# Sums of the first projection on VectorE, the fourth product's input in two halves, other banks for the values' upper half

## The chip, the cores and the metric

One core of one Trainium2 chip runs one program. The metric is the device time of one execution in microseconds (us), as the median of several runs. A row of the trace gives times from the start of the profiled execution's span.

## The reference, cut to what matters

A decoder block on 1024 tokens of width 1024: a projection, attention with forgetting and a spatial gate side by side, an output projection, then a gated MLP with a convolution. The change lies in the first quarter, where the projections are made and the gate begins:

```python
xn = rmsnorm(h, norm_mix_g)
proj = xn @ w_in                      # q, k, v (512 each), u, vg (512 each), 8 forget columns
uv = jax.nn.gelu(proj[..., V_END:G_END])
u, vg = uv[..., :512], uv[..., 512:]
vg = rmsnorm(vg, v_gain)              # per group of 64
mixed = einsum('gij,bnjgd->bnigd', tril(w_s), vg) + b_s
sg = u * mixed
```

## The kernel before, in words

**Arithmetic.** A matrix product in float32 is made from three products in a faster format: each operand is split into a high part (a rounded copy, made by ScalarE) and a low part (the operand less the high part, made by VectorE), and TensorE adds high by high, high by low and low by high. `split_w` makes such a pair of a weight, `own` and `hl_of` make it of the tokens' side; `tsplit` (L246) takes a buffer from a ring of six (`ring`, two buffers named wy and four named whl) and splits into it.

**The first projection** (columns u and vg) splits tokens and columns into halves and needs seven products instead of eight. They run one after another: B11, B21, then T2, T3, T1, T4 and B22. A product is 48 matmuls: four blocks `k` of the summed dimension, four blocks of tokens (a PSUM bank each) and three parts. `tmul` issues the twelve of one `k`. The operands called T2, T3, T1 and T4 are sums and differences of blocks: on the tokens' side made from `tmp`, on the weights' side in `sum23` (VectorE), `sum4` (GpSimd) and a loop of four GpSimd additions over `gb`. T3 is the fourth product counted from B11. Between B21 and T2 the value columns are multiplied for the first half of the tokens (`values_low`, eight groups of twelve matmuls, 264 columns wide); after B22 they are multiplied for the other half (`values_high`, the same size, for 256 value columns and the 8 forget columns). Later in the program the other 256 value columns follow (VH for the second half of the tokens, VL for the first).

**PSUM.** There are eight banks, four under the tag "b" (`bank`) and four under "s" (`sbank`). The seven products take them in turn by fours, under the names B and S; `values_high` gets four new "s" banks. `ut[1]` is the last result of B22: VectorE reads it out of the "s" banks (L478, `ut[1] = B[m] - ut[1]`), and only then are these banks free again. In the four steps of the query and key projections (`qk_step`, `product`), `psq` gives tags a and b to "b" banks, c and d to "s" banks.

**Other work beside the products.** The mean squares of the tokens' rows come from eight loads of `xtok`, in turn into one buffer named t01 and one named pt, with a square on ScalarE behind each. t01 is first free when `own("T1", ...)` has read it. From the sums come `rstd1`, and then the gelus of `ut` and `vgt`, the gate's squares, and `gate_norm`.

**Second half of the value columns and the gate's start.** `w0` holds the split weights. The order is VH T3, VL B21, `head_loads(0)` (loads of the first attention head, the last of which needs the buffer of the B21 tokens), VL B11, evacuation of VL, `kept(1)` (load of the values kept in memory since `values_high`, and their evacuation by `evac_v` into tiles named V, which take the buffers of the B11 tokens), VH B22, and `spatial()`: it splits the spatial weights into `ws` (both tiles named wy), evacuates VH, loads the table for Exp, and multiplies the eight groups of the gate, in four banks.

**What sets the order.** A scheduler orders each engine's instructions by the program's order and its own estimate of when each is ready, and gives out buffers and waits. The class `Line` overrides it: while `act.on` and `dve.on` are set, ScalarE and VectorE each run their instructions strictly in the program's order; later ones come behind the last of these. `after`, `behind` and `seq` add single orders. Instructions recorded through `Line` show L51 while the order is on and L44 when it is off, so those line numbers are helpers'. L259 is the matmul of `tmul`, L365 the loads of xtok, L720 to L722 the gate's matmuls, L744 transposes of the gated output, L328 and L353 the GpSimd sums.

Of the kernel before, what the change touches and what calls it, by code (L numbers as in the profile page):

```python
# [14 lines left out]
P = 128  # L15
# [50 lines left out]
def block_kernel(ctx: ExitStack, tc: tile.TileContext, xT, xtok, wuv, wv0, wv1, wqk, cpk, bfv,  # L66
# [16 lines left out]
    def nm(s):  # L83
        uid[0] += 1
        return f"{s}_{uid[0]}"
# [103 lines left out]
    def xr(n, k):  # L189
        return RAW[n][k // 2][:, k % 2, :]  # L190
# [8 lines left out]
    def ring(dt=F32R, n=512):  # L199
        rn[0] += 1  # L200
        return sb(RTAG[(rn[0] - 1) % 6], [P, 2, n], dt)

    def psq(tag):
        return psa.tile([P, 512], F32, tag="b" if tag in "ab" else "s", bufs=4, name=nm("q" + tag))

    def own(n, src, k, row):

# [35 lines left out]
    vgt = [sb("G", [P, 4, 512]) for _ in range(2)]  # L243
    ut = [sb("A", [P, 4, 512]) for _ in range(2)]

    def tsplit(src, gate=None, n=512):  # L246
        w = ring(n=n)
        d = split_w(src, (w[:, 0], w[:, 1]))
        if gate:
            behind(d, gate)  # L250
        return w

    def tmul(banks, w, n, k, first, apart=False, ms_=range(4), own=True):

        ops = [(m, c) for m in ms_ for c in range(3)]
        for m, c in sorted(ops, key=lambda o: (o[1] > 0, o)) if apart else ops:
            ms = slice(m * P, (m + 1) * P)
            xi, wi = ((0, 0), (0, 1), (1, 0))[c]
            pe.matmul(banks[m], xs(n, xi, k)[:, ms], w[:, wi, :], start=(first and k == 0 and c == 0 and (own or m % 2 == 0)),  # L259
                      stop=(k == 3 and c == 2), skip_group_check=True)  # L260
# [30 lines left out]
    def keep(banks, hf):  # L291
        t = ring(F32).rearrange("p a (b c) -> p (a b) c", c=256)
        for m in range(4):
            act.copy(t[:, m, :], banks[m][:, 0:256])
            act.copy(zf[:, 4 * hf + m, 0:8], banks[m][:, 256:264])
        sp.dma_start(out=vd[hf], in_=t)
# [16 lines left out]
    for m in range(4):  # L313
        dve.tensor_tensor(out=ut[0][:, m, :], in0=S[m], in1=vgt[0][:, m, :], op=ALU.add)
    values_low(3)
    act.on = dve.on = False

    s2 = []

    def sum23(k):  # L320
        a11, a21, a22 = ua[k][:, 0, :], gb[k][:, 0, :], gb[k][:, 1, :]
        s2.append(sb("gg", [P, 512]))
        dve.tensor_tensor(out=a11, in0=a21, in1=a11, op=ALU.add)
        dve.tensor_tensor(out=s2[k], in0=a11, in1=a22, op=ALU.add)

    def sum4(k):
        a12 = ua[k][:, 1, :]
        return pool.tensor_tensor(out=a12, in0=s2[k], in1=a12, op=ALU.add)  # L328

    sum23(0)  # L330
    sum23(1)
    for k in range(4):
        tmul(S, tsplit(s2[k]), "T2", k, True)
        s4 = sum4(k)
        if k < 2:
            sum23(k + 2)
    keep(B, 0)
    B, S = S, B

    for j in range(2):  # L340
        t1, t2, t3 = tmp[j]
        for c in range(2):
            k = 2 * j + c
            dve.scalar_tensor_tensor(out=t3[:, c], in0=xr("x12", k), scalar=gk(k), in1=t3[:, c],
                                     op0=ALU.mult, op1=ALU.subtract)
    XS["B22"] = xset(("t3", "t2"))
    for k in range(4):
        own("B22", xr("x22", k), k, 4 + k)
    XS["T3"] = xset(("x1", "x2"))
    for j in range(2):  # L350
        hl_of("T3", j, tmp[j][2])
    for w in gb:
        after(tc, pool.tensor_tensor(out=w[:, 0, :], in0=w[:, 0, :], in1=w[:, 1, :], op=ALU.add), s4)  # L353
    tprod(S, lambda k: ua[k][:, 0, :], "T3", True)
    for m in range(4):
        dve.tensor_tensor(out=ut[1][:, m, :], in0=B[m], in1=vgt[0][:, m, :], op=ALU.subtract)
    XS["T1"] = xset(("H", "H"))
    for j in range(2):
        for c in range(2):
# [11 lines left out]
    sp.dma_start(out=rb, in_=rbd.rearrange("a b -> (a b)").unsqueeze(0).to_broadcast((P, 1024)))  # L371

    tprod(B, lambda k: gb[k][:, 0, :], "T1", True)
    for m in range(4):
        dve.tensor_tensor(out=vgt[1][:, m, :], in0=ut[1][:, m, :], in1=S[m], op=ALU.add)
    for j in range(2):
# [79 lines left out]

    gate_part(1, 0)
    gate_part(1, 2)
    S = [sbank() for _ in range(4)]

    def values_high(k):
        t = wh[k]
# [46 lines left out]
    def forget_sums(c, r):  # L509
        bfb, z, e = c[:, 136:144], c[:, 144:208], c[:, 208:272]  # L510
        tri, ones, lh, ll = r[:, 0:P], r[:, P:2 * P], r[:, 256:320], r[:, 320:384]
        v3 = lambda t: t.rearrange("p (h t) -> p h t", h=8)
        dve.tensor_tensor(out=v3(z), in0=zf[:, :, 0:8].rearrange("p t h -> p h t"),
                          in1=rstd1.unsqueeze(1).to_broadcast((P, 8, 8)), op=ALU.mult)
        dve.tensor_tensor(out=v3(z), in0=v3(z), in1=bfb.unsqueeze(2).to_broadcast((P, 8, 8)), op=ALU.add)
        dve.scalar_tensor_tensor(out=e, in0=z, scalar=-1.0, in1=z, op0=ALU.mult, op1=ALU.max)
        act.activation(e, e, AF.Exp, scale=-1.0)
        act.activation(e, e, AF.Ln, bias=one[:, 0:1])
        dve.tensor_scalar(out=z, in0=z, scalar1=-1.0, scalar2=0.0, op0=ALU.mult, op1=ALU.max)
        dve.tensor_tensor(out=z, in0=z, in1=e, op=ALU.add)  # L520
        dve.tensor_copy(lh, z)
        dve.tensor_tensor(out=ll, in0=z, in1=f32(lh), op=ALU.subtract)
        yield
        ps = sbank()
        for o, m in ((64, tri), (128, ones)):
            pe.matmul(ps[:, o:o + 64], m, lh, start=True, stop=False)
            pe.matmul(ps[:, o:o + 64], m, ll, start=False, stop=True)
        whole, run = v3(ps[:, 128:192]), v3(e)
        dve.memset(run[:, :, 0:1], 0.0)
        for tt in range(1, 8):  # L530
            dve.tensor_tensor(out=run[:, :, tt:tt + 1], in0=run[:, :, tt - 1:tt], in1=whole[:, :, tt - 1:tt], op=ALU.add)
        dve.tensor_tensor(out=v3(z), in0=v3(ps[:, 64:128]), in1=run, op=ALU.add)

        yield
        pe.transpose(ps[0:64, 192:320], z, ident)
        rows = c[0:64, 272:400]
        act.activation(rows, ps[0:64, 192:320], AF.Copy, scale=-1.0)
        sp.dma_start(out=ncr.rearrange("h (t p) -> (h t) p", p=P), in_=rows)
        yield
# [92 lines left out]
        sp.dma_start(out=t, in_=wv1[k])  # L632
        wvr.append(t)

    w0 = [tsplit(wvr[k].rearrange("p a b -> p (a b)"), "keys" if k < 2 else "queries") for k in range(4)]


    gate_gain(0)
# [24 lines left out]
                                 in1=f32(v[:, :, 0, :]), op0=ALU.mult, op1=ALU.subtract)  # L663

    def kept(hf):
        t = ring(F32).rearrange("p a (b c) -> p (a b) c", c=256)
        sp.dma_start(out=t, in_=vd[hf])
        for j in range(4):
            if j % 2 == 0:
                V.append(sb("V", [P, 2, 8, 2, 64], F32R))  # L670
            evac_v(4 * hf + j, 0, t[:, j, :])
# [28 lines left out]
        splits[:] = [split_w(wr, (w[:, 0], w[:, 1]), hi, "pool")]  # L700
        return w

    def spatial():

        wr = sb("pt", [P, 8, P])
        sp.dma_start(out=wr, in_=wsp)
        pool.affine_select(out=wr, in_=wr, pattern=[[0, 8], [1, P]], compare_op=ALU.is_ge,
                           fill=0.0, base=0, channel_multiplier=-1)
        ws = [sb("wy", [P, 8, P], F32R) for _ in range(2)]
        act.on = dve.on = True  # L710
        split_w(wr, ws)

        act.activation(pad[:, 0:1], eps, AF.Exp)
        for m in range(4):
            evac_v(4 + m, 1, VH[m])
        tmp = [sb("pt", [P, 4, 256]) for _ in range(2)]
        for g in range(8):
            c, j = g // 2, g % 2
            ps = bank()
            pe.matmul(ps, ws[0][:, g, :], vgs[c][:, 0, j], start=True, stop=False)  # L720
            pe.matmul(ps, ws[0][:, g, :], vgs[c][:, 1, j], start=False, stop=False)
            m = pe.matmul(ps, ws[1][:, g, :], vgs[c][:, 0, j], start=False, stop=True)  # L722
            v3 = lambda t: t.rearrange("p (t d) -> p t d", d=64)
            u = [ut[hf][:, :, g * 64:(g + 1) * 64] for hf in range(2)]
            dve.scalar_tensor_tensor(out=u[0], in0=v3(ps[:, 0:256]), scalar=bs[:, g:g + 1], in1=u[0],
                                     op0=ALU.add, op1=ALU.mult)
            t = tmp[g // 4][:, g % 4, :]

            def second():
                act.activation(t, ps[:, 256:512], AF.Identity, bias=bs[:, g:g + 1])  # L730
                x = pool.tensor_tensor(out=u[1], in0=v3(t), in1=u[1], op=ALU.mult)
                after(tc, x, splits[0])

            if g < 7:
                second()
        seq(m)
        return second

# [35 lines left out]
    for k in range(4):  # L774
        tmul(VH, a1[k], "T3", k, True, own=False)
    for k in range(4):
        tmul(VL, w0[k][:, :, 256:512], "B21", k, True, own=False)
    for k in range(4):
        pool.tensor_tensor(out=wvr[k][:, 1, :], in0=wvr[k][:, 0, :], in1=wvr[k][:, 1, :], op=ALU.add)
    loads, rows = [None] * 8, [None] * 8  # L780
# [20 lines left out]

    head_loads(0)
    for k in range(4):
        tmul(VL, a1[k], "B11", k, False)
    for m in range(4):
        evac_v(m, 1, VL[m])
    kept(1)
    for k in range(4):
        tmul(VH, tsplit(wvr[k][:, 1, :], n=256), "B22", k, False)
    whs, wrs = [], sg_load(0)  # L810
    for s in range(2):
        after(tc, sp.dma_start(out=ncd[s].rearrange("h (t p) -> (h t) p", p=P), in_=sums[1 + s]), queued[0])
# [836 lines left out]
```

## Time and profile before

| what | value |
|---|---|
| median of 3 runs | 1078.75 us (1078.75 to 1079.66) |
| profiled execution, its own time | 1078.43 us |
| its span, first to last instruction | 1076.7 us |
| TensorE clock granted, mean | 0.992 |
| busy: TensorE, weight loads, VectorE, ScalarE, GpSimd | 98%, 82%, 83%, 53%, 23% |

A row of the timeline gives start, length, engine, line, operation, output<-inputs, shapes and count; in brackets stands the idle time before it and what ended it. Rows of several instructions (x24) are merged. A matmul's end is modelled, so consecutive rows of TensorE are read by their starts. PE is TensorE, DVE VectorE, ACT ScalarE, POOL GpSimd, and SPq the queue from which most transfers are issued.

### The profile page before, as it was taken

The page shows a single profiled execution, that of the slowest core. Times are in us where ns is not written, and L with a number is a line of the kernel's source. Part 1 is how long each engine was busy: PE and PEld are TensorE (multiplying, and loading weights), DVE is VectorE, ACT ScalarE, POOL GpSimd, SP SyncE. Part 2 cuts the span into 40 slices and gives each one's busy share as a digit, 9 for nine tenths or more (in the row PEclk, how much of TensorE's full clock was granted, in tenths as well). Part 3 has the DMA queues.
Part 4 walks back from the last instruction along what each step waited for, and adds up shares of the span by engine and source line. Part 5 has one row for each costly group of instructions (what it writes and reads, how often), then busy time and mean ns, then how long its engine had stood idle before and what let it go on. Part 6 is the DMA issues. An engine that isn't in the chain of part 4 may idle for free.

```text
span 1076.7 us, 14627 instructions
## 1 busy us (share of the span) xinstructions
PE 1054.3 (98%) x5156; PEld 885.6 (82%) x5156; DVE 888.9 (83%) x1291; ACT 571.8 (53%) x1015; POOL 247.6 (23%) x185
## 2 busy tenths in 40 slices
PE   9898999989999999999999999999999999999997
PEld 7877888978898987887888888888888888888886
DVE  6986697876777868999899999989988776898774
ACT  6468544465767755754444444444444444454653
POOL 0502232340402551044333333333322000000000
PEclk9989999999999999999999999999999999999999
DMA  9054166736656345232244513323331899433442
GB/s 339 38 163 132 61 167 175 220 103 189 181 157 181 117 155 180 75 117 98 98 137 153 178 66 132 98 94 103 108 112 45 289 332 313 125 98 96 141 125 96
DMA packets 67184, 155.78 MB, mean 145 GB/s; under 512 B 9028, under 2 KB 9748, under 8 KB 67112
## 3 DMA queue, kind: packets, MB, share of 16 engines
q1 hardware_dynamic: 65800, 154.82, 44.9%
q8 instruction: 40, 0.66, 0.3%
q14 instruction: 32, 0.26, 0.1%
q10 hardware_dynamic: 1312, 0.04, 0.1%
HBM read 111.96 MB, written 42.87 MB: 144 GB/s over the span
## 4 chain that ended last, share of the span: by engine, by line
PE 84%; DVE 8%; DMA 3%; ACT 3%; issue 2%; SPq 0%; POOL 0%; ACTq 0%; DVEq 0%; POOLq 0%
PE k L1499 19%; PE qa L1241 11%; PE qc L1241 10%; PE qd L1241 10%; PE qb L1241 5%; PE pb L938 3%; PE ps L259 3%; PE pb L919 3%; PE qa L406 2%; PE qc L406 2%; PE qd L406 2%; PE pl L879 2%; PE pl L880 2%; PE pf L963 1%; PE pf L965 1%
## 5 line engine op out<-in xcount | busy, mean ns | idle before, releaser
L1499 PE MATMUL k<-whb,wha 128*128 128x512 f32 x924 | 209.7, 389 | 0.0
L1499 PEld LDWEIGHTS k<-whb,wha 128*128 128x128 f32 x924 | 173.4, 188 | 36.2 <-DVE wha L161 0.2
L1241 PE MATMUL qc<-xT,whb 128*128 128x512 f32 x540 | 129.9, 389 | 0.5 <-DVE u L1352 0.5
L1241 PE MATMUL qa<-xB,wha 128*128 128x512 f32 x528 | 127.2, 390 | 0.0
L1241 PEld LDWEIGHTS qc<-xT,whb 128*128 128x128 f32 x540 | 101.2, 188 | 22.1 <-DVE u L1352 0.9
L1241 PEld LDWEIGHTS qa<-xB,wha 128*128 128x128 f32 x528 | 98.8, 188 | 20.8 <-DVE wha L161 0.4
L155 ACT CAST wha<-sg 128x512 fp32r<-128x512 f32 x77 | 47.8, 622 | 96.8 <-PE k L1499 86.3
L155 ACT CAST whb<-sg 128x512 fp32r<-128x512 f32 x82 | 50.5, 617 | 86.8 <-PE qc L1241 68.3
L161 DVE TENSOR_TENSOR wha<-sg,wha 128x512 fp32r<-128x512 f32 x77 | 52.7, 687 | 41.6 <-ACT wha L155 41.5
L920 ACT CAST pt<-pb 128x512 fp32r<-128x512 f32 (+1 forms) x80 | 42.2, 544 | 43.1 <-PE pb L919 34.3
L1241 PE MATMUL qd<-xB,whb 128*128 128x512 f32 x264 | 63.9, 390 | 0.1
L1241 PE MATMUL qd<-xT,whb 128*128 128x512 f32 x264 | 63.6, 389 | 0.0
L1128 POOL TENSOR_TENSOR sg<-raw 128x512 f32<-128x512 f32 x20 | 30.1, 1506 | 136.3 <-DVE whb L161 75.7
L161 DVE TENSOR_TENSOR whb<-sg,whb 128x512 fp32r<-128x512 f32 x82 | 57.7, 704 | 4.4 <-ACT whb L155 4.3
L1241 PE MATMUL qb<-xT,whb 128*128 128x512 f32 x252 | 60.8, 389 | 0.0
L921 DVE TENSOR_TENSOR pt<-pb,pt 128x512 fp32r<-128x512 f32 (+1 forms) x80 | 48.8, 634 | 12.3 <-ACT pt L920 11.0
L1241 PEld LDWEIGHTS qd<-xB,whb 128*128 128x128 f32 x264 | 49.5, 188 | 10.7 <-DVE h L1360 0.5
L1241 PEld LDWEIGHTS qd<-xT,whb 128*128 128x128 f32 x264 | 49.6, 188 | 10.3
L1241 PEld LDWEIGHTS qb<-xT,whb 128*128 128x128 f32 x252 | 47.3, 188 | 9.8
L938 PE MATMUL pb<-pt,V 128*128 128x256 f32 x320 | 52.1, 287 | 0.3 <-DVE pt L921 0.2
L1131 POOL TENSOR_TENSOR sg<-sg,raw 128x512 f32<-128x512 f32 x20 | 33.3, 1665 | 64.2 <-DVE whb L161 64.2
L1129 POOL TENSOR_TENSOR sg<-sg,raw 128x512 f32<-128x512 f32 x20 | 34.9, 1744 | 50.7 <-issue 48.8
(399 smaller groups left out, 2311.1 us busy)
## 6 DMA issues: line engine op xcount, KB each, us to landing
raw<-wup SPq DMA_DIRECT2D x44, 512.0 KB
sg<-hx SPq DMA_DIRECT2D x77, 256.0 KB
hx<-hs SPq DMA_DIRECT2D x44, 256.0 KB
hx<-ca SPq DMA_DIRECT2D x35, 256.0 KB
xT<-wdn SPq DMA_DIRECT2D x28, 256.0 KB
x<-kd SPq DMA_DIRECT2D x24, 256.0 KB
raw<-wqk SPq DMA_DIRECT2D x8, 512.0 KB
qd<-G SPq DMA_DIRECT2D x16, 256.0 KB
```

The costliest lines, as they stand in the source:

```text
L155: act.copy(h, src)
L161: return eng.tensor_tensor(out=l, in0=src, in1=f32(h), op=ALU.subtract)
L259: pe.matmul(banks[m], xs(n, xi, k)[:, ms], w[:, wi, :], start=(first and k == 0 and c == 0 and (own or m % 2 == 0)), stop=(k == 3 and c == ...
L406: pe.matmul(ps, w[:, wi, ks], xs(n, xi, k), start=(first and c == 0), stop=(c == 11), skip_group_check=True)
L919: seq(pe.transpose(ptr[:, c:c + P], tj[jj][:, k * P:(k + 1) * P], ident))
L920: casts.append(act.copy(pt[:, 0, 0:w], ptr[:, 0:w]))
L921: los.append(dve.tensor_tensor(out=pt[:, 1, 0:w], in0=ptr[:, 0:w], in1=f32(pt[:, 0, 0:w]), op=ALU.subtract))
L938: seq(pe.matmul(po[0][:, oo:oo + n], lhs, pt[:, s, o:o + n], start=(k == 0 and s == 0), stop=(s == 1 and half)))
L1129: pool.tensor_tensor(out=s[1], in0=s[0], in1=a11, op=ALU.add)
L1131: pool.tensor_tensor(out=s[3], in0=s[1], in1=a12, op=ALU.add)
L1241: pe.matmul(ps, w[:, wi, ks], xb[:, xi, k, :], start=(first and n == 0), stop=(n == 11), skip_group_check=True)
L1499: pe.matmul(banks[bk + m], xh[:, xi, ms], wh[:, wi, :], start=(first and p_ == 0 and n == 0), stop=(p_ == NP - 1 and n == 2), skip_group_c ...
```

## The change

It has five parts.

1. `sum4` and the four sums of `gb` go from GpSimd to VectorE. `sum4` of the first two `k` comes between the T2 weights, that of the others behind T1's weights; the `gb` sums come behind T3.
2. The strict order of ScalarE and VectorE, which ended after `values_low(3)`, now lasts until T3's weights are split. T3's token side (`third`) is made in two halves, each directly ahead of its two weights; the tokens' side of B22, which was made ahead of T3, is made there too.
3. `values_high` and the forget gate's sums take "b" banks instead of "s"; in `psq` the two tags change places.
4. VL B11 now runs ahead of VL B21.
5. The load of `kept(1)` goes to a buffer named G; the splitting of the spatial weights is taken out of `spatial` and put, with `kept(1)`, ahead of the evacuation of VL; in `spatial`, VH's last two evacuations come behind the first two groups, and the Exp table's load behind VH's first two.

```diff
     def psq(tag):
-        return psa.tile([P, 512], F32, tag="b" if tag in "ab" else "s", bufs=4, name=nm("q" + tag))
+        return psa.tile([P, 512], F32, tag="s" if tag in "ab" else "b", bufs=4, name=nm("q" + tag))
...
-    def tsplit(src, gate=None, n=512):
-        w = ring(n=n)
+    def tsplit(src, gate=None, n=512, tag=None):
+        w = sb(tag, [P, 2, n], F32R) if tag else ring(n=n)
...
     values_low(3)
-    act.on = dve.on = False
...
     def sum4(k):
         a12 = ua[k][:, 1, :]
-        return pool.tensor_tensor(out=a12, in0=s2[k], in1=a12, op=ALU.add)
-
-    sum23(0)
-    sum23(1)
-    for k in range(4):
-        tmul(S, tsplit(s2[k]), "T2", k, True)
-        s4 = sum4(k)
-        if k < 2:
-            sum23(k + 2)
-    keep(B, 0)
-    B, S = S, B
-
-    for j in range(2):
+        dve.tensor_tensor(out=a12, in0=s2[k], in1=a12, op=ALU.add)
+
+    def third(j):
         t1, t2, t3 = tmp[j]
         for c in range(2):
             k = 2 * j + c
             dve.scalar_tensor_tensor(out=t3[:, c], in0=xr("x12", k), scalar=gk(k), in1=t3[:, c],
                                      op0=ALU.mult, op1=ALU.subtract)
-    XS["B22"] = xset(("t3", "t2"))
-    for k in range(4):
-        own("B22", xr("x22", k), k, 4 + k)
-    XS["T3"] = xset(("x1", "x2"))
+        if not j:
+            XS["B22"] = xset(("t3", "t2"))
+        for c in range(2):
+            own("B22", xr("x22", 2 * j + c), 2 * j + c, 4 + 2 * j + c)
+        if not j:
+            XS["T3"] = xset(("x1", "x2"))
+        hl_of("T3", j, tmp[j][2])
+
+    sum23(0)
+    sum23(1)
+    tmul(S, tsplit(s2[0]), "T2", 0, True)
+    tmul(S, tsplit(s2[1]), "T2", 1, True)
+    for k in (2, 3):
+        sum4(k - 2)
+        sum23(k)
+        tmul(S, tsplit(s2[k]), "T2", k, True)
+    keep(B, 0)
+    B, S = S, B
     for j in range(2):
-        hl_of("T3", j, tmp[j][2])
-    for w in gb:
-        after(tc, pool.tensor_tensor(out=w[:, 0, :], in0=w[:, 0, :], in1=w[:, 1, :], op=ALU.add), s4)
-    tprod(S, lambda k: ua[k][:, 0, :], "T3", True)
+        third(j)
+        for k in (2 * j, 2 * j + 1):
+            tmul(S, tsplit(ua[k][:, 0, :]), "T3", k, True)
+    act.on = dve.on = False
     for m in range(4):
         dve.tensor_tensor(out=ut[1][:, m, :], in0=B[m], in1=vgt[0][:, m, :], op=ALU.subtract)
+    for w in gb:
+        dve.tensor_tensor(out=w[:, 0, :], in0=w[:, 0, :], in1=w[:, 1, :], op=ALU.add)
...
     tprod(B, lambda k: gb[k][:, 0, :], "T1", True)
+    sum4(2)
+    sum4(3)
...
-    S = [sbank() for _ in range(4)]
+    S = [bank() for _ in range(4)]
     def values_high(k):
...
-        ps = sbank()
+        ps = bank()
...
-    w0 = [tsplit(wvr[k].rearrange("p a b -> p (a b)"), "keys" if k < 2 else "queries") for k in range(4)]
+    w0 = [tsplit(wvr[k].rearrange("p a b -> p (a b)"), "keys" if k < 2 else "queries", tag="whl") for k in range(4)]
...
     def kept(hf):
-        t = ring(F32).rearrange("p a (b c) -> p (a b) c", c=256)
+        t = sb("G" if hf else "wy", [P, 4, 256])
...
-    def spatial():
-
+    def spatial_weights():
         wr = sb("pt", [P, 8, P])
...
         ws = [sb("wy", [P, 8, P], F32R) for _ in range(2)]
+        split_w(wr, ws)
+        return ws
+
+    def spatial():
+
         act.on = dve.on = True
-        split_w(wr, ws)
-
+        for m in range(2):
+            evac_v(4 + m, 1, VH[m])
         act.activation(pad[:, 0:1], eps, AF.Exp)
-        for m in range(4):
-            evac_v(4 + m, 1, VH[m])
...
             if g < 7:
                 second()
+            if g in (0, 1):
+                evac_v(6 + g, 1, VH[2 + g])
...
     for k in range(4):
-        tmul(VL, w0[k][:, :, 256:512], "B21", k, True, own=False)
+        tmul(VL, a1[k], "B11", k, True, own=False)
...
     head_loads(0)
     for k in range(4):
-        tmul(VL, a1[k], "B11", k, False)
+        tmul(VL, w0[k][:, :, 256:512], "B21", k, False)
+    kept(1)
+    ws = spatial_weights()
     for m in range(4):
         evac_v(m, 1, VL[m])
-    kept(1)
     for k in range(4):
-        tmul(VH, tsplit(wvr[k][:, 1, :], n=256), "B22", k, False)
+        tmul(VH, tsplit(wvr[k][:, 1, :], n=256, tag="whl"), "B22", k, False)
```

## The prediction, made before the changed kernel was run

> **What bounds the kernel now.** I read the page first, then TensorE's waits up to 240 us, its timeline there, the clock by stretches, and the other engines' timelines around each wait.
>
> ```profile
> PE 1054.3 (98%) x5156; PEld 885.6 (82%) x5156; DVE 888.9 (83%) x1291; ACT 571.8 (53%) x1015; POOL 247.6 (23%) x185
> ```
>
> TensorE is busy almost throughout; a gain must come out of its few waits. All of any size before the end lie where the change is made:
>
> ```profile
> PE pb L259 <- ACT x L44: 3.0, 1, 3.0
> PE ps L259 <- DVE A L44: 2.9, 1, 2.9
> PE pb L720 <- ACT pt L51: 2.5, 1, 2.5
> PE pb L259 <- DVE whl L44: 1.5, 1, 1.5
> PE pb L722 <- DVE wy L51: 1.0, 1, 1.0
> ```
>
> In order: T3's tokens, the banks of the values' upper half, banks in the gate, T3's weights, the gate's weights. A wait costs more than its length where the clock falls behind it:
>
> ```profile
> 106.00:108.00 2.00, 2.00 (x11) 1.82 (x10) 1.97 (x4) 1.17 (x3) 2.00 (x2) 0.54 0.00 0
> 220.00:222.00 2.00, 0.96 (x6) 0.46 (x4) 1.97 (x4) 0.00 (x0) 0.00 (x0) 1.00 1.02 203
> ```
>
> The columns are the stretch, its length, five engines' busy time, the granted clock, the DMA share and GB/s. After the 2.9 us wait the clock is 0.54; the 1.0 us wait at 221 leaves it at 1.00. TensorE's rows give each place its cost:
>
> ```profile
> 39.97 5.60 PE L259 MATMUL ps<-whl,H 128*128 128x512 f32 x24
> 45.41 5.60 PE L259 MATMUL ps<-wy,H 128*128 128x512 f32 x24
> 54.00 0.50 PE L259 MATMUL pb<-whl,x 128*128 128x512 f32 x1 [3.00 <-ACT x L44]
> 55.99 10.95 PE L259 MATMUL pb<-whl,x 128*128 128x512 f32 x35 [1.48 <-DVE whl L44]
> 69.49 2.88 PE L259 MATMUL ps<-wy,H 128*128 128x512 f32 x12
> 99.41 2.88 PE L259 MATMUL ps<-wy,t 128*128 128x512 f32 x12
> 105.17 2.13 PE L259 MATMUL ps<-wy,x 128*128 128x264 f32 x9 [2.88 <-DVE A L44]
> 117.24 1.60 PE L259 MATMUL ps<-whl,t 128*128 128x264 f32 x12
> 118.68 2.93 PE L406 MATMUL qa<-V,whl 128*128 128x512 f32 x12
> 213.16 5.92 PE L259 MATMUL ps<-whl,t 128*128 128x256 f32 x48
> 218.92 0.40 PE L720 MATMUL pb<-H,wy 128*128 128x512 f32 x1
> 225.70 0.79 PE L720 MATMUL pb<-H,wy 128*128 128x512 f32 x1 [2.53 <-ACT pt L51]
> 230.09 1.91 PE L744 MATMUL ps<-ident,A 128*128 128x128 f32 x16
> ```
>
> By the starts, 24 matmuls take 45.41 - 39.97 = 5.44 us, a product 10.88. T2 ends at 45.41 + 5.44 = 50.85, T1 begins at 69.49: T3 takes 18.64, which is 7.8 too long. B22 ends at 99.41 + 2.72 = 102.13. A group of the values' upper half takes 118.68 - 117.24 = 1.44, eight take 11.5; they took 118.68 - 105.17 = 13.5, so the slow clock cost 2.0 besides the 2.9. The gate's 24 matmuls, 5.44 at full speed, take from 218.92 to 230.09, 11.2. So 7.8 + 4.9 + 5.7 = 18.4 us is the most to be had.
>
> **The change part by part. T3.** VectorE and GpSimd before:
>
> ```profile
> 44.84 6.82 POOL L353 TENSOR_TENSOR G<-G 128x512 f32<-128x512 f32 x4
> 32.98 1.28 DVE L44 TENSOR_TENSOR raw<-G,raw 128x512 f32<-128x512 f32 x2
> 43.65 1.78 DVE L44 SCALAR_TENSOR_TENSOR pt<-t,g,pt 128x512 f32<-128x512 f32 x1
> 54.12 1.21 DVE L44 TENSOR_TENSOR x<-pt,x 128x1024 fp32r<-128x1024 f32 x1
> 58.80 2.47 DVE L44 TENSOR_TENSOR A<-ps,G 128x512 f32<-128x512 f32 x4
> 62.52 1.40 DVE L44 SCALAR_TENSOR_TENSOR H<-t,g,H 128x512 fp32r<-128x512 f32 x2
> 50.56 1.33 ACT L44 ACTIVATE t<-x,g 128x512 fp32r<-128x512 f32 x2 [3.25 <-DVE G L44]
> 52.90 1.04 ACT L44 CAST x<-pt 128x1024 fp32r<-128x1024 f32 x1 [1.01 <-DVE t L44]
> ```
>
> A three-operand step takes 1.78 us beside GpSimd's additions and 0.70 (half of 1.40) without them. An addition takes 0.6 on VectorE (1.28 for two, pipelined), 1.7 on GpSimd. So moving the sums shortens what stands beside them. In the strict order VectorE goes on at 32.98. Four sums and two low parts bring it to about 36.9 (estimate, with the waits for ScalarE's high parts). Two rounds of `sum4`, two sums, a high part (0.65) and a low part are 3.3 each: 43.5. Each half of T3 is then 1.4 (two steps), 0.8 (ScalarE's first scaled copy), 1.4 (two low parts of B22's tokens), 1.1 (the 1024 copy), 1.2 (its low part) and 1.2 (two weights) = 7.1: 50.6 and 57.7. The first half is there when T2 ends at 50.85. The second half's first weight is complete at 57.2 where TensorE wants it at 50.85 + 5.44 = 56.3: a wait of about 1.0, too short for the clock by the row at 221. T3 ends at 62.7, 6.8 earlier.
>
> **T1, a new wait.** Before T1's first low part VectorE still has T2's readout (2.4 by the row at 58.80), the `gb` sums that GpSimd did unseen (2.4), four low parts of T1's tokens (2.8, by 62.52) and the weight (0.6). From 57.8 that is 66.0. TensorE waits about 3.1 us and, by the 2.9 us wait above, loses 2.0 more to the clock. T1 ends at 78.7, T4 at 89.6, B22 at 100.4. The other two `sum4` (1.2) are hidden by T1's 10.9 us; T4's tokens would be ready at 77.5 in my count, so without that cover they cost little.
>
> The Trainium skill ("TensorE: Matmul & The Clock Gate", section "Part 1: The HAM clock gate") puts the fall to half clock behind an idle window of about 3.4 us. By it the wait of 2.88 would have cost only itself, and the sum below would be 2.0 smaller, 1072.7. The row at 106, 0.54 after 2.88 us, speaks against it here, and I take the row.
>
> **The values' upper half.** The new banks were read after T4, so B22's readout no longer holds TensorE. What comes next is the chain behind the mean squares:
>
> ```profile
> 63.94 0.33 SPq L365 DMA_DIRECT2D t<-xtok  x1
> 78.88 4.21 DMA t<-xtok
> 88.36 2.56 ACT L44 ACTIVATE A<-A,rstd 128x512 f32<-128x512 f32 x4
> 100.12 0.42 DVE L44 TENSOR_TENSOR wy<-G,wy 128x264 fp32r<-128x264 f32 x1
> 104.34 2.48 DVE L44 TENSOR_TENSOR A<-ps,A 128x512 f32<-128x512 f32 x4
> 109.39 0.76 DVE L44 TENSOR_TENSOR wy<-G,wy 128x264 fp32r<-128x264 f32 x2
> ```
>
> Four loads through t01 (first at 63.94, last landing at 83.1) lead to the gelus at 88.36, and the first low part of these weights comes at 100.54 on VectorE behind gate work that hangs on them. T1's token parts now end at 65.4 instead of 63.9, so t01 comes 1.5 later and the low part at 102.0. The groups then run to 102.0 + 11.5 = 113.5, against 118.68: **5.2 us gained at the front.** The wait of 1.6 is between the two seen above; I take the clock as kept. The swapped tags in `psq` only move the readout of B22 (104.34 to 106.8) ahead of the first query product at 113.5, with 7 us to spare. The 28 products that follow run without a wait now and carry the gain on.
>
> **The gate.**
>
> ```profile
> 217.75 2.89 DVE L44 SCALAR_TENSOR_TENSOR V<-wy,rstd,V 128x256 fp32r<-128x256 f32 x4 [2.28 <-ACT V L44]
> 220.68 1.23 DVE L51 TENSOR_TENSOR wy<-pt,wy 128x1024 fp32r<-128x1024 f32 x1
> 215.82 1.28 ACT L51 ACT_TABLE_LOAD   x1
> 225.17 1.65 ACT L51 ACTIVATE pt<-pb,cp 128x256 f32<-128x256 f32 x4 [0.94 <-DVE A L51]
> 207.59 0.45 SPq L797 DMA_DIRECT2D x<-kd  x1
> ```
>
> In today's times: VectorE evacuates the kept values until 220.6, splits the gate's weights until 221.9, and only then reads VH; the first bank is free again at about 225.6. With B11 first, the V buffers come free where B21's tokens do now (the last head load goes out behind them at 207.59), and both jobs fit under the two products up to 218.9. From 218.4, VH's first two evacuations (0.5 each on either engine, one after another, since they share a bank) and the table's 1.28, which was hidden at 215.82 and now is not, bring the first bank's release to 222.0. TensorE's first four groups end at 221.7, so it waits 0.3; the two late evacuations delay the next two banks to 223.7 and 225.4, waits of 1.1 each. The transposes begin at 227.0 instead of 230.1: 3.1 gained. If the load of the kept values is issued behind the head's last load (now at 207.59, then at 213.3, where B21's tokens are released), it is about 0.6 less. I take 2.8, between 0 and the 5.7 above.
>
> **The sum.** 1078.43 (the profiled execution: span 1076.7 and 1.7 around it) - 5.2 - 2.8 = 1070.4. The runs' median is 0.3 higher: **1070.7 us**. Behind 234 us nothing changes, and TensorE's near-full load carries the gain to the end.
>
> **The rivals.**
>
> *VectorE keeps its order in the upper half.* Today the fifth and sixth weights' low parts come at 109.39, behind the gate's normalization. If the scheduler puts them there again, 1.5 later, at 111.3, TensorE, which wants the fifth at 102.0 + 5.8 = 107.8, waits 3.5 us and loses 2.0: end near 119, front gain 0, 1076.0. For it: the row. Against it: TensorE now reaches these buffers earlier, so the scheduler may see them ready before the gate's work. 0.17.
>
> *The front gains in full.* T1's parts are interleaved, or the squares are not late: no wait at T1, 1.0 or less at the values, 9 to 11 us in front: about 1066. Against it stands the count of VectorE's work. 0.12.
>
> *The gate gains nothing:* the kept values' load lands late behind the transfers that B21's release holds back, and the split waits with it as now: 1073.6. For it: the queue runs in order. Against: the weights' split needs no such load. 0.10.
>
> *Slower: the chain of squares slips.* Each round through t01 takes about 5 us (63.94 to 78.88 for three). Every us of slip goes into the start of the upper half, and once TensorE waits there as long as today, 2.0 more for the clock: the end is 100.5 + 11.5 + 2.0 = 114.0 and the slip. It decides from a slip of 7.4 us (4.6 eat the front gain, 2.8 the gate's; 1.5 is forecast). If t01 comes 3 us later still, because the new sums push T1's tokens back, and each of four rounds takes 1.5 longer beside the casts, the slip is 10.5, the end 124.5, the front 5.8 lost: 1082. 0.08.
>
> **How the numbers follow.** The forecast has 0.53. The range of 8 in 10 goes from 1065.5, taking in most of the full front gain, to 1076.2 with the kept order; outside stay the slip and a part of the ends. A measurement of this kernel tells about 0.2%, 2.2 us, from no change: faster means below 1076.6. All cases but the slip end there, though the kept order only just; a third of it is counted as the same: faster 0.86, same 0.06, slower 0.08.
>
> **What would show it.** Right: no wait of T3's matmuls over 1.5 us, T1 beginning near 66 behind a wait for VectorE, the upper half at 102 with no wait for `ut[1]`, the first query product near 113.5, no GpSimd between 2 and 75 us, the table load between VH's evacuations, the transposes 8 us after VH's product. Wrong: T1's matmuls start at once, T3's second half comes after 58, the upper half's fifth weight is waited for, or the kept values are still read after VH's product.

## The result and the profile after

The changed kernel took 1069.82 us (median of 4 runs, 1067.95 to 1071.9) against 1078.75 (1077.36 to 1079.66): a ratio of 0.9919 [0.9898, 0.994]. The prediction said 1070.7, from 1065.5 to 1076.2. Two further sets of runs gave 1070.94 (0.9924 [0.9912, 0.9935]) and 1068.74 (0.9906 [0.9894, 0.9919]). The profiled execution shown here is the slowest of its four, 1071.9 us with a span of 1070.2.

TensorE is busy for 1051.8 us of it (98%), against 1054.3 before. TensorE's waits up to 240 us (waiting engine and line, what ended the wait, total us, times, longest):

```profile
PE ps L259 <- DVE wy L44: 2.2, 1, 2.2
PE pb L729 <- ACT pt L51: 1.6, 2, 0.8
...
PE pb L259 <- DVE whl L44: 1.1, 1, 1.1
PE pb L259 <- ACT whl L44: 0.8, 1, 0.8
```

T3's wait of 3.0 us for its tokens, the 2.9 us for the banks of the upper half and the gate's 2.5 us are gone. New are T1's first weight (2.2), the second group of the upper half (0.8 and 1.1) and two short waits in the gate. TensorE's timeline shows where they lie:

```profile
57.26 2.79 PE L259 MATMUL pb<-whl,x 128*128 128x512 f32 x11 [0.84 <-DVE whl L51]
...
62.60 1.07 PE L259 MATMUL ps<-wy,H 128*128 128x512 f32 x4
65.92 3.03 PE L259 MATMUL ps<-wy,H 128*128 128x512 f32 x8 [2.25 <-DVE wy L44]
...
77.67 2.88 PE L259 MATMUL pb<-whl,V 128*128 128x512 f32 x12
...
99.43 1.61 PE L259 MATMUL pb<-wy,x 128*128 128x264 f32 x12
101.84 0.39 PE L259 MATMUL pb<-whl,t 128*128 128x264 f32 x1 [0.80 <-ACT whl L44]
103.32 1.90 PE L259 MATMUL pb<-whl,t 128*128 128x264 f32 x11 [1.09 <-DVE whl L44]
...
114.96 2.93 PE L413 MATMUL qa<-V,whl 128*128 128x512 f32 x12
...
215.20 0.40 PE L729 MATMUL pb<-H,wy 128*128 128x512 f32 x1
...
223.18 1.91 PE L755 MATMUL ps<-ident,A 128*128 128x128 f32 x16
```

T1 begins at 62.60 instead of 69.49, B22 ends at 99.43 instead of 102.13, the first query product begins at 114.96 instead of 118.68, and from VH's end to the transposes it is 223.18 - 215.20 = 7.98 us instead of 11.17. From the 6.9 us of T1's start, 3.7 are left at the first query product (0.57 of them an earlier T2, 39.40 against 39.97, which the change doesn't touch); the gate adds 3.2. Behind it nothing moves: from the first matmul of the attention's logits (233.54 before, 226.67 after) to the end of the span it is 843.2 and 843.5 us. The clock by stretches (stretch, length, busy time of five engines, granted clock, DMA share, GB/s) tells where the front's gain went:

```profile
66.00:68.00 2.00, 2.00 (x7) 1.55 (x8) 2.00 (x4) 0.00 (x0) 0.00 (x0) 0.72 0.87 336
68.00:70.00 2.00, 2.00 (x6) 1.55 (x5) 2.00 (x4) 1.66 (x3) 0.00 (x0) 0.50 0.39 156
...
104.00:106.00 2.00, 2.00 (x13) 2.00 (x12) 2.00 (x4) 1.92 (x4) 1.37 (x1) 0.60 0.74 269
106.00:108.00 2.00, 2.00 (x12) 2.00 (x12) 2.00 (x4) 1.46 (x4) 1.92 (x3) 0.54 0.03 3
```

The clock falls to half behind T1's 2.25 us and again behind the upper half's 0.80 and 1.09. So in this execution the front gained 3.7 us, where the forecast had 5.2, and the gate 3.2, where it had 2.8. The chain behind the mean squares, on the queue, ScalarE and VectorE:

```profile
65.29 0.33 SPq L370 DMA_DIRECT2D t<-xtok  x1
...
87.08 1.06 ACT L44 ACTIVATE t<-t 128x1024 f32<-128x1024 f32 x1 [2.88 <-DMA t<-xtok]
...
88.56 0.43 DVE L44 TENSOR_TENSOR wy<-G,wy 128x264 fp32r<-128x264 f32 x1 [2.40 <-ACT wy L44]
...
102.84 1.11 DVE L44 TENSOR_TENSOR whl<-G,whl 128x264 fp32r<-128x264 f32 x3
```

The first low part of the upper half's weights now comes at 88.56, ahead of the gate's work; the three others of the first four come at 102.84, behind it. So the first group runs on arrival, and the second waits for the chain.

### The profile page after: what moved, and what is told of

Same layout as the page of the kernel before. It is cut to its first block, busy times and chain, and to the rows that moved or that the text cites. A ratio compares the mean times of both kernels' runs of the same rounds, so it can differ in the third digit from the quotient of the medians.

```text
span 1070.2 us, 14618 instructions
## 1 busy us (share of the span) xinstructions
PE 1051.8 (98%) x5156; PEld 882.8 (82%) x5156; DVE 885.3 (83%) x1299; ACT 570.4 (53%) x1014; POOL 234.7 (22%) x177
## 4 chain that ended last, share of the span: by engine, by line
PE 88%; DVE 6%; ACT 2%; issue 1%; DMA 1%; SPq 0%; ACTq 0%; DVEq 0%
PE k L1511 20%; PE qa L1253 11%; PE qc L1253 10%; PE qd L1253 10%; PE qb L1253 5%; PE pb L259 4%; PE ps L259 4%; PE pb L950 3%; PE pb L931 3%; PE qa L413 2%; PE qc L413 2%; PE qd L413 2%; PE pl L891 2%; PE pl L892 2%; PE pf L975 1%
```

## The experiments

All times are medians; "before" ran beside each set. "Gain" is taken from the ratio, in us of 1078.5. A profile shows one execution of a set, not its median.

**Which part brings what.** The change was taken apart into its front (parts 1 and 2), the banks (part 3) and the gate (parts 4 and 5), each put alone into the kernel before:

```diff
# e1_front, with the rest of parts 1 and 2
     values_low(3)
-    act.on = dve.on = False
...
+            tmul(S, tsplit(ua[k][:, 0, :]), "T3", k, True)
+    act.on = dve.on = False
# e2_banks, with the tags of psq
-    S = [sbank() for _ in range(4)]
+    S = [bank() for _ in range(4)]
# e3_gate, with the rest of parts 4 and 5
+    kept(1)
+    ws = spatial_weights()
```

> Only the sums on VectorE, T3's two halves and the longer strict order; old banks, old second half. My theory (the start of the values' upper half is set by the chain of squares and by VectorE's queue, not by when TensorE arrives): T3 ends about 7 us earlier, T1 waits 2 to 3 us with half clock behind it, TensorE comes to the upper half some 2 us earlier and waits that much longer there for the readout of B22: next to no gain, 1078 with a spread of 1.5. Rival (each microsecond taken out of T3 is passed on): the 2.7 us by which T1 ended earlier in the full change stay, 1076.

Measured: 1075.94 against 1078.48, ratio 0.9971 [0.996, 0.9982]. TensorE's timeline:

```profile
101.38 0.73 PE L413 MATMUL qa<-V,whl 128*128 128x512 f32 x2 [1.53 <-ACT whl L44]
103.00 1.40 PE L413 MATMUL qa<-V,whl 128*128 128x512 f32 x5 [0.89 <-DVE whl L44]
104.24 0.52 PE L259 MATMUL ps<-wy,x 128*128 128x264 f32 x3
```

The upper half did begin at 104.24, held by its banks as in the kernel before. But the scheduler put seven matmuls of the first query product into that wait, and the clock stayed at 1.00 behind it, where the kernel before had 0.54. The front alone gains 3.1 us: the number was the rival's (1076) and not my theory's (1078), and I had not foreseen that an empty place is filled. The profile is of the fastest of the ten executions (1073.15 us), so it doesn't show how often the clock is kept there.

> Only the exchanged banks. VectorE's order is as before, so the low part of the upper half's fifth weight still stands behind the gate's normalization (near 109.4). My theory: the upper half starts at 102.1 without a wait, TensorE waits about 2 us at the fifth weight with some of the clock behind it; the first query product begins near 116, gain 1.5 to 3, 1076.5. Rival (the bank wait was the whole loss): 2.9 of the wait and 2.0 of the clock come back, first query product at 113.8, 1074. Other rival (the wait only moves to the first query product): it waits for the readout of B22, no gain.

Measured: 1076.78, ratio 0.998 [0.9971, 0.9989].

```profile
100.74 1.92 PE L259 MATMUL pb<-wy,x 128*128 128x264 f32 x12
...
110.34 2.76 PE L259 MATMUL pb<-wy,x 128*128 128x264 f32 x11 [2.89 <-DVE wy L44]
...
117.68 2.93 PE L406 MATMUL qa<-V,whl 128*128 128x512 f32 x12
```

The upper half began at 100.74 without a wait for its banks, and then the fifth group waited 2.89 us for VectorE: this is the place of the prediction's first rival, "VectorE keeps its order". The changed kernel has no wait there. The banks alone move the wait: it is as long as before, and the first query product came only 1.0 us earlier in this profile, the slowest of its set (1077.93).

> Only the second half's order of products, the kept values' other buffer, the early split of the gate's weights and the evacuations in the gate; old front. My theory: the gate's transposes begin 8.0 us behind the end of VH's product instead of 11.2, gain 3.2, 1075.5, as this place stands by itself. Rival (the head's loads, held back by B21's later release, cost it again in the attention): gain under 1.

Measured: 1076.73, ratio 0.998 [0.9971, 0.9989]. From VH's end to the transposes it took 8.59 us, with the clock at half behind the last short wait:

```profile
225.08 0.51 PE L722 MATMUL pb<-H,wy 128*128 128x512 f32 x1 [0.82 <-ACT pt L51]
226.34 0.63 PE L723 MATMUL pb<-H,wy 128*128 128x512 f32 x1
...
227.19 2.93 PE L748 MATMUL ps<-ident,A 128*128 128x128 f32 x16
```

A matmul of 0.63 us where the others take 0.39 is the fallen clock (0.50 from 226 to 228). The gate part works alone, with a gain of 2.2 us where I expected 3.2.

> The changed kernel as it is, for the sum of the parts on the same chip and for its spread. My theory: 1069.8 again, within 1.5; front and banks together 5 to 6, the gate 3.2. If the parts simply add, their gains sum to this one's; by my theory front and banks together give more than the two apart, since each alone leaves the other's wait standing.

Measured: 1070.94, ratio 0.9924 [0.9912, 0.9935], the profile's first query product at 113.42; this is the first repetition of the changed kernel. The three parts alone give 3.1 + 2.2 + 2.2 = 7.5 us, the whole 8.2 in the same set.

**Front and banks together.** Do they need each other?

```diff
# against the changed kernel: parts 4 and 5 undone
-        tmul(VL, a1[k], "B11", k, True, own=False)
+        tmul(VL, w0[k][:, :, 256:512], "B21", k, True, own=False)
```

> Both parts of the front together (sums on VectorE, the strict order with T3 in halves, the other banks), the gate as in the kernel before. Theory (the front parts need each other: alone, the order still waits for the banks at 104.2 us and the banks still wait for VectorE's fifth low part at 110.3): the first query product comes at 114 to 115.5 us, the gain is 5.2 to 6.5 us, that is 1071.5 to 1073.0 beside a before of 1078.3, more than the 2.5 and 1.7 of the two alone. Rival (the parts only add up): 4.2 us or less, 1074.0 or more, the first query product at 116 or later.

Measured: 1072.59, ratio 0.9952 [0.9936, 0.9967], runs from 1070.74 to 1077.57. That is 5.2 us where the two alone give 5.3. The median lies in the range of my theory and the ratio at its lower end, but the ratios add up as the rival says, and the first query product of the profile (116.44) is where the rival put it: with this spread neither is shown. The profile is of the slowest run, and it shows one thing that can spread the times:

```profile
66.42 2.11 PE L259 MATMUL ps<-wy,H 128*128 128x512 f32 x8 [2.24 <-DVE wy L44]
...
98.84 1.61 PE L259 MATMUL pb<-wy,x 128*128 128x264 f32 x12
102.06 0.39 PE L259 MATMUL pb<-whl,t 128*128 128x264 f32 x1 [1.60 <-ACT whl L44]
103.53 2.79 PE L259 MATMUL pb<-whl,t 128*128 128x264 f32 x11 [1.09 <-DVE whl L44]
...
116.44 2.93 PE L413 MATMUL qa<-V,whl 128*128 128x512 f32 x12
```

Here T1's wait of 2.24 us left the clock at 1.00, TensorE came to the upper half earlier than in the changed kernel (98.84 against 99.43), and waited the longer there (1.60 and 1.09 us): the second group's eleven matmuls started at 103.53 all the same, and the clock lost behind it cost more.

> The changed kernel again, beside the two others on the same chip. Both theories: 1070 to 1071.5; the first query product at 113.4 to 115.

Measured: 1068.74, ratio 0.9906 [0.9894, 0.9919], faster than expected. Its row for the second group, and that of the first repetition:

```profile
102.22 1.59 PE L259 MATMUL pb<-whl,t 128*128 128x264 f32 x11 [0.19 <-DVE whl L44]
...
112.29 2.93 PE L413 MATMUL qa<-V,whl 128*128 128x512 f32 x12
```

```profile
103.33 1.60 PE L259 MATMUL pb<-whl,t 128*128 128x264 f32 x11 [1.09 <-DVE whl L44]
...
113.42 2.93 PE L413 MATMUL qa<-V,whl 128*128 128x512 f32 x12
```

From the second group's row to the first query product it is 10.07 and 10.09 us at full clock, 11.64 in the first profile of the change and 12.91 in the front with banks: 1.6 and 2.8 us lost to the clock. The row itself follows the last square by 16.2 us in all four (87.08 to 103.32, 87.09 to 103.33, 87.30 to 103.53, 85.98 to 102.22). So in these four the end of the front is the last square + 16.2 + 10.1 + what the clock loses, and T1's wait and its lost clock are not in it: TensorE came at 98.84, 99.43, 99.88 and 100.30, and the earliest ended last. The sum holds only as long as one group stands ahead of the gate's work and TensorE is there before the second group's weight; the orders below change both.

**What VectorE does behind T3.** Four orders of the same work, in place of the end of the strict order. VectorE's order is kept, ScalarE's ends:

```diff
-    act.on = dve.on = False
+    act.on = False
...
# e6_blocks: the gb sums and T1's tokens and weights in this order
+    gb_sum(0)
+    own_t1(0)
+    t1_mul(0)
+    gb_sum(1)
+    own_t1(1)
+    dve.on = False
# e7_tokens_first
+    own_t1(1)
+    own_t1(0)
+    for k in range(4):
+        gb_sum(k)
+    dve.on = False
# e8_both
+    gb_sum(0)
+    own_t1(1)
+    w = tsplit(gb[0][:, 0, :])
+    own_t1(0)
+    tmul(B, w, "T1", 0, True)
+    dve.on = False
# e9_tokens_late
+    for k in range(4):
+        gb_sum(k)
+    own_t1(0)
+    t1_mul(0)
+    t1_mul(1)
+    sum4(2)
+    sum4(3)
+    own_t1(1)
+    dve.on = False
```

`gb_sum(k)` is one of the four sums of `gb`, `own_t1(j)` makes T1's tokens of half `j`, `t1_mul(k)` splits a weight of T1 and multiplies it. In e6 and e8 the other sums follow between T1's weights. `own_t1(1)` is the one that reads t01, so t01 is free when it has run.

> The changed kernel with VectorE's work ahead of T1 put in the order in which T1 needs it, block by block: T2's readout, the first gb sum, the first half of T1's tokens, the first weight's low part, then the rest; t01 comes free about when it did. My theory (the chain of squares sets the start of the values' upper half): T1's wait of 2.2 us and the half clock behind it go, TensorE comes to the upper half about 4 us earlier and waits that much longer there, so 1 us or less is gained, 1069 to 1071. Rival (TensorE's arrival sets it): the 4 us are kept, 1066.

Measured: 1070.26 against 1077.85, ratio 0.9937 [0.9923, 0.995].

```profile
75.85 2.97 PE L259 MATMUL pb<-whl,V 128*128 128x512 f32 x12 [2.31 <-ACT t L44]
...
100.34 0.39 PE L259 MATMUL pb<-whl,t 128*128 128x264 f32 x1 [1.03 <-ACT whl L44]
```

T1's wait went to T4 (2.31 us), and the upper half waited about as long as in the changed kernel (1.03 and 1.09 us). The last square came at 85.58 and the second group's eleven matmuls 16.2 us behind it, as above; the clock fell behind the two waits (0.62 and 0.53 from 102 to 106), and the first query product came at 113.45, against 113.42 in the first repetition. Taking T1's wait away brought nothing by itself: the ratio is no better than the changed kernel's three.

> The changed kernel with both halves of T1's tokens ahead of the gb sums, the half that frees t01 first; T1's first weight is complete when it was. My theory: T1 waits as long as in the changed kernel, but the loads through t01 begin 3.8 us earlier and with them the gelus, so the upper half's waits (0.8 and 1.1, with half clock in some executions) go: the first query product begins at 111 instead of 113.4 to 115, 1067 to 1068. Rival (TensorE's arrival sets the upper half's start): no change, 1070.5.

Measured: 1068.54, ratio 0.9913 [0.9899, 0.9926].

```profile
65.15 3.02 PE L259 MATMUL ps<-wy,H 128*128 128x512 f32 x12 [2.27 <-ACT wy L44]
...
81.13 1.06 ACT L44 ACTIVATE t<-t 128x1024 f32<-128x1024 f32 x1 [1.25 <-DMA t<-xtok]
...
110.66 2.93 PE L424 MATMUL qa<-V,whl 128*128 128x512 f32 x12
```

T1 waits as long as in the changed kernel, but the last square comes at 81.13 instead of 87.08 and the front ends at 110.66, with the clock at 1.00. The squares are 6 us earlier and the front, against the first repetition, only 2.8: now the upper half starts where B22 ends (98.10) and runs with a single wait of 0.67 us at its seventh group, so it is mainly TensorE's arrival that sets the end, and no longer the squares. In time, all four runs (up to 1069.44) lie below the five of e6_blocks (from 1069.97), which ran beside them; against the changed kernel's 0.9924, 0.9919 and 0.9906 the gain isn't shown. The profile is of the fastest run, 1066.91.

> Both at once: the first gb sum, the half of T1's tokens that frees t01, the first weight, the other half, then the rest. My theory: T1's wait is gone, t01 comes free 3 us earlier, the upper half starts near 98 and the first query product near 110: 1065 to 1067, and more than the gains of the two orders apart. Rival (VectorE's total work sets the end of the upper half whatever the order): 1070.

Measured: 1067.55, ratio 0.9904 [0.989, 0.9917]. It has the lowest median of the four orders, with no wait at T1, 2.24 us at T4 (VectorE's readout of T3) and the first query product at 110.98. But the intervals of e7_tokens_first and e9_tokens_late overlap with its own, and 1065 to 1067 was expected: that both together bring more than each apart isn't shown. It was run again:

> The version without T1's wait, a second time. Theory (the front ends where the chain of squares and VectorE's order let the upper half begin, about 2 us earlier than in the changed kernel, and the falls of the clock decide the rest): a ratio of 0.989 to 0.9915 to the kernel before, the first query product at 110.5 to 112.5 us. Rival (the better time of its first set was chance, the changed kernel's three sets were 0.9906 to 0.9924): 0.9915 or more, the first query product at 113 or later.

Measured: 1066.86 against 1078.24, ratio 0.9892 [0.9876, 0.9909].

```profile
109.76 2.93 PE L427 MATMUL qa<-V,whl 128*128 128x512 f32 x12
```

It beats the kernel before by about 1% in both sets. Against the changed kernel (0.9924, 0.9919, 0.9906) it is ahead each time, but the two never ran in one set and the intervals touch.

> The other way round: the half of T1's tokens that frees t01 comes behind the first two weights and two sums, some 2.5 us later than in the changed kernel; T1's first weight is complete 1.3 us earlier. My theory (the chain of squares): the upper half is fed 2.5 us later, 1072 to 1073. Rival (arrival): T1 waits 1.3 us less, 1069.

Measured: 1068.12, ratio 0.991 [0.9896, 0.9924]; here my theory fell and the rival's number held.

```profile
68.06 0.33 SPq L385 DMA_DIRECT2D t<-xtok  x1
87.57 1.06 ACT L44 ACTIVATE t<-t 128x1024 f32<-128x1024 f32 x1 [2.53 <-DMA t<-xtok]
```

t01 came 2.8 us later than in the first profile of the changed kernel, but the last square only 0.5 later. The rounds are not of one length: from t01's first load to the last square it is 19.5 us here and 21.8, 21.3 and 19.8 in the three profiles of the changed kernel. And two of the upper half's weights were split ahead of the chain (at 85.07 and 90.66), so that the second group ran on arrival and the third was the one to wait (0.98 us). With the latest square of all orders and 0.9 us of wait at T1 the front ended at 111.78. So the squares alone don't set it either: by these rows, how many weights VectorE splits ahead of the chain counts as well.

**The sums themselves.**

```diff
-        dve.tensor_tensor(out=a12, in0=s2[k], in1=a12, op=ALU.add)
+        return pool.tensor_tensor(out=a12, in0=s2[k], in1=a12, op=ALU.add)
...
-        dve.tensor_tensor(out=w[:, 0, :], in0=w[:, 0, :], in1=w[:, 1, :], op=ALU.add)
+        after(tc, pool.tensor_tensor(out=w[:, 0, :], in0=w[:, 0, :], in1=w[:, 1, :], op=ALU.add), s4)
```

The last two `sum4` stand ahead of T3 again, not behind T1's weights.

> The changed kernel with all eight sums back on GpSimd; order, halves, banks and gate stay changed. Theory (GpSimd's additions slow VectorE's steps beside them, 1.78 us against 0.70): the additions run from about 36 to 58 us, the three-operand steps of T3 take 1.2 to 1.8 us each, T3's second half is waited for 3 to 6 us instead of 0.8, T3 ends at 65 to 68; T1 then starts without a wait of its own, since 2.4 us of sums are gone from VectorE there, so the front ends at most 2 us later: 1070 to 1073. Rival (the additions on GpSimd cost VectorE little): T3's wait stays under 1.5 us, T1's wait of 2.25 us is gone or under 0.5, T4 and the squares come 2 us earlier, 1068 to 1069.5.

Measured: 1072.12, ratio 0.9943 [0.9931, 0.9955], beside 1068.74 for the changed kernel in the same set: 3.4 us slower, and still 6.1 us of gain over the kernel before. Rows of VectorE, GpSimd and TensorE:

```profile
36.95 1.54 DVE L51 TENSOR_TENSOR whl<-gg,whl 128x512 fp32r<-128x512 f32 x1 [0.16 <-ACT whl L51]
45.16 3.48 DVE L51 SCALAR_TENSOR_TENSOR pt<-t,g,pt 128x512 f32<-128x512 f32 x2
44.64 6.81 POOL L363 TENSOR_TENSOR G<-G 128x512 f32<-128x512 f32 x4
53.65 0.80 PE L259 MATMUL pb<-whl,x 128*128 128x512 f32 x1 [3.37 <-ACT whl L51]
55.00 10.71 PE L259 MATMUL pb<-whl,x 128*128 128x512 f32 x35 [0.55 <-DVE whl L51]
```

Two three-operand steps take 3.48 us beside the additions and 1.41 in the changed kernel (43.57 there), a low part 1.54 instead of 0.69. T3 waits 3.9 us in all, in the bounds of the theory, but for its first half, not the second: the additions were over by 51.5, earlier than I had counted. The clock is at 0.50 from 54 to 60 besides, and T3 takes 68.26 - 50.28 = 18.0 us. T1 then has no wait (2.88 for its first twelve at 68.26), while the changed kernel pays its 2.25 us and 1.9 of clock there, so little of this is left in front: the first query product comes at 113.70, 1.4 us behind the 112.29 of the changed kernel's profile of the same set and 0.3 behind that of the first repetition. Another 1.0 of the 3.1 us between the two profiles of this set lies in the gate, where the clock fell here (8.98 us against 7.97), as it did in the first repetition with the sums on VectorE. The Trainium skill ("GPSIMD Engine Reference", section "1. Specifications") says that GpSimd shares its SBUF interfaces with VectorE, and that instructions with two SBUF inputs contend; these rows agree, at 2.5 times for the three-operand step.

## Why the prediction was right

The time came out 0.9 us from the forecast, but not by the forecast's own steps everywhere: in the front, misses cancel.

- **T3: right.** The second half waits 0.84 us (1.0 predicted) and T3's last twelve end at 62.60 (62.7). The end owes something to luck: T2 ended 0.57 us earlier, and T3 took 12.3 us where 11.9 were forecast. The steps that stood beside GpSimd's additions take 1.41 for two, as counted from the row at 62.52 of the kernel before. No GpSimd instruction runs between 2 and 75 us. Putting the sums back costs 3.4 us in one set, of which the profiles show 1.4 in the front.
- **T1's new wait: right in place, a bit smaller.** The first weight is complete at 65.9 (66.0). Four matmuls run ahead, the wait is 2.25 us instead of 3.1 and the clock costs 77.67 - 62.60 - 10.88 - 2.25 = 1.9 (2.0). TensorE is 1.0 us ahead of the forecast when B22 ends, 99.43 against 100.4.
- **The upper half: the right number by errors that cancel.** The step "t01 comes 1.5 later and the low part at 102.0" failed. The last square comes at 87.08, 4.0 us later and not 1.5, against this row of the kernel before:

```profile
83.10 1.06 ACT L44 ACTIVATE t<-t 128x1024 f32<-128x1024 f32 x1 [3.74 <-DMA t<-xtok]
```

  Of the 4.0 us, 1.35 are t01, as counted, and the rest is four rounds that took 21.8 us instead of 19.2. My slower rival, the slipping chain, so came true for 4.0 of the 7.4 us at which it decides. Two things stood against it. The scheduler split the first weight ahead of the gate's work, so only seven groups stand behind the chain and not eight: 1.44 us back. And the stretch from the last square to the low part that TensorE waits for was 16.2 us, where the kernel before took 17.4 (83.10 to 100.54), with two casts, 1.1 us together, between its gelus: 1.2 us back. At full clock that ends at 113.4, where I had put 113.5: this is luck. With what the clock lost it was 114.96 here, and 113.42 and 112.29 in the repetitions.
- **The clock: too sure.** "The wait of 1.6 is between the two seen above; I take the clock as kept" failed in the first profile: waits of 0.80 and 1.09 us, 1.5 apart, brought it to 0.54 and cost 1.6 us. In the first repetition the same place, with waits of 0.37 and 1.09, kept it:

```profile
106.00:108.00 2.00, 2.00 (x19) 2.00 (x18) 2.00 (x4) 2.00 (x5) 1.92 (x3) 1.00 0.00 0
222.00:224.00 2.00, 2.00 (x10) 1.70 (x9) 0.51 (x2) 0.75 (x2) 1.66 (x3) 0.52 0.49 179
```

  The second row is the gate of that repetition: there the clock fell where the first profile kept it. A single length of wait from which the clock falls, as the forecast used it, isn't in these runs. (The forecast's row at 220 ends together with the wait of 1.0 us that it was read for; the stretches of 1 us behind it, 222 to 225, show 1.00 too, so that reading holds.)
- **The banks and the gate: right.** Nothing waits for `ut[1]` any more. In the gate the waits are 0.2, 0.82 and 0.82 (0.3, 1.1 and 1.1 predicted), and the order is as foreseen:

```profile
204.00 1.23 DVE L44 TENSOR_TENSOR wy<-pt,wy 128x1024 fp32r<-128x1024 f32 x1
211.67 1.67 DVE L44 SCALAR_TENSOR_TENSOR V<-G,rstd,V 128x256 fp32r<-128x256 f32 x4
216.20 1.28 ACT L51 ACT_TABLE_LOAD   x1
```

  The weights are split and the kept values read under the two products, and the table's load lies between VH's evacuations. The gain is 3.2 us at full clock (2.8 taken) and 2.2 where the clock falls (8.93 us instead of 7.98 in the first repetition).
- **The rivals.** "VectorE keeps its order" is what the banks alone do (2.89 us at the fifth group). "The front gains in full" needs the squares early: it is nearest in e14_both, whose first query product comes 8.9 us earlier than in the kernel before. "The gate gains nothing" did not happen.

Open stay three things. Whether the parts do more together than alone: 7.5 us against 8.2 to 10.1 for the whole lies within the intervals. What the place of the sums is worth by itself: 3.4 us by the medians of one set, 1.4 by the front of its profiles. And what decides a fall of the clock behind a short wait: the outcome varies between profiles at nearly equal waits, and no experiment set its phase.

## What to carry to other kernels

When a wait is taken away, ask which chain the next one hangs on, and follow it back to its first transfer: here the loads of the squares, released by VectorE's last step of T1's tokens, set the end of the front in the changed kernel, and every us that TensorE gained ahead of them it spent waiting for them. As long as a later wait is fixed by another chain, a wait in front of it costs nothing, its lost clock included, so don't add up prices along one engine when a second chain decides. Once that chain is fast enough, as in e7_tokens_first, TensorE's own arrival counts again. And where short waits stand close together, keep both prices for the clock in the range.

## What was not expected of the hardware

- The clock's answer to equal waits differs. T1's wait of 2.25 us brought 0.72 and 0.50 in the changed kernel; 2.24 us left it at 1.00 in the front with banks, 2.27 in e7_tokens_first. Waits of 0.80 and 1.09 us with 0.4 us of work between them were enough for 0.54. The Trainium skill ("TensorE: Matmul & The Clock Gate", section "Part 1: The HAM clock gate") says that the window of activity runs free of the kernel's start, and that the length of the slow start varies with its phase. Differing outcomes behind equal waits would fit such a window, though no run here shows its phase; falls behind waits of about 1 us, far under the window of some 3.4 us that the Trainium skill gives there, do not follow from its idle rule.
- GpSimd's additions cost VectorE more than VectorE takes to do them. Eight additions of 0.6 us are 4.8 us on VectorE. On GpSimd they made the steps beside them, from 34 to 52 us, some 6 us longer than the same steps in the changed kernel (3.48 and 2.58 for two three-operand steps instead of 1.41 and 1.42, 1.66, 1.54 and twice 1.2 for single steps instead of 0.69).
- The rounds of loads vary: 19.8 to 21.8 us from t01's first load to the last square in three profiles of the same kernel, so that t01's time alone doesn't give the last square's.
